# A hybrid decoder layer on one core: the merged blocks' sums change engine, low halves and transfers change place

## The chip, the cores and the metric

The kernel runs on one core of one Trainium2 chip. The metric is the device time of one execution in microseconds. Three timed runs of the kernel before stand beside one profiled execution, in which the hardware profiler recorded the instructions of every engine. The engines are TensorE (PE, with its weight loads PEld), VectorE (DVE), ScalarE (ACT), GpSimd (POOL) and SyncE (SP), whose queue starts nearly all DMAs here.

## The reference

One layer of a decoder with two token mixers side by side, 1024 tokens of width 1024, all in float32:

```python
h = rmsnorm(x, norm_g)
proj = h @ w_in                              # q, k, v, gates, decay code, merge logits
o_gla = gla_chunked(g_q, g_k, g_v, log_a)    # gated linear attention, 4 heads
o_gla = rmsnorm(o_gla, gla_norm_g) * silu(g_gate)
y_a = o_gla @ w_pa
o_sb = stick_breaking(s_q, s_k, s_v)         # 8 heads, strictly causal
o_sb = o_sb * silu(s_gate)
y_b = o_sb @ w_pb
gates = sigmoid(m_logits + b_gate)
merged = gates[0] * y_a + gates[1] * y_b
x = x + merged @ w_o
return rmsnorm(x, final_g)
```

The stick-breaking weight of key s for query t is beta[t, s] times the product of (1 - beta[t, j]) over s < j < t, with beta = sigmoid(q k / sqrt(d)).

## The kernel before, in words

**Numbers in two halves.** TensorE multiplies in a reduced form of float32. So every operand is split: ScalarE writes a high half (`activation(hi, src, Copy)`), VectorE subtracts it and writes a low half (`tensor_sub(lo, src, hi)`), and a product is three matmuls, high by high, high by low, low by high. The helper `split` (L164 to L166) does both; the last stage has its own, `o_hi` (L1188 on) and `o_lo` (L1192 on).

**Strassen blocks.** Large products are made from 2 x 2 blocks with seven products in place of eight, in Winograd's form: combinations S1 to S4 of one operand's blocks A11 to A22, combinations T1 to T4 of the other's blocks B11 to B22. A product of one unit is 12 matmuls of 128x512 (4 pieces of the contraction, three matmuls each).

**The stages, in order of time.**

1. The first rows of x are normalised (square on ScalarE, `norm_a`, with a first step of its reciprocal root on VectorE and the power on POOL; `norm_b` scales), transposed, split, and multiplied with the first value weights (L424 to L459). ScalarE and VectorE run in the order of the program here; the low halves of the first block are at L441, the low half of the first weights at L442.
2. Further values (L516 on), with the sums S1 to S4 of h.
3. "Pairs": 28 jobs of seven units (`Pairs.run`), each job a projection of 256 columns. While they run, other work is laid between the units: first the decay (22 slots), then the T sums of the two later weights w_pb and w_o (`tjobs`, L729 on: `t_load`, `t_sum`, `t_store`, one slot per unit), up to unit GLA_AT, then the GLA steps, four units to a step. TensorE's order is a scheduler's there; ScalarE's and VectorE's is the program's until the T sums end.
4. The stick-breaking heads (L1088 on), 8 heads of 8 steps. Step i of head h computes the scores of a later step, transposes the weights of block i (`turn`, tags tr and pp, high half ath or afh, low half atl or afl), and at two of the steps the values (`values`, bank av). Units of other projections are laid between by SB_PLAN. The order of all engines is a scheduler's.
5. The last stage (L1110 on), where ScalarE, VectorE and TensorE run in the order of the program: 28 items multiply the stick-breaking output by w_pb (`a_product`) and merge it with the other branch under the gates (`a_merge`), leaving merged blocks A11, A12, A21 and A22 in four quarters each; 28 further items multiply the merged blocks by w_o (`item`), add the residual (`add`), square for the norm (`square`), scale and store. An item is one product. I number them through, 0 to 55, so that 28 is the first of w_o.

**What sets the order in the last stage.** The table `parts` says at which item which operand is split, `loads` at which item which operand is loaded. In each item first the adds of finished products run (`evict_a`), then the low halves of this item (`los`), then the high halves of the next (`his`). Before the change, the merged sums S1, S3, S2 are made on POOL in the items 24 to 27 and S4 in 28 to 31 (`sums`, with `nc.gpsimd.tensor_tensor` in it, L1152); S4 and S3 go through DRAM (`d_s`) and come back by `o_load`. The low halves of A12 are made in the items 28 to 31, mixed with those of T2 and S2:

```python
28: [("T2", (0,)), ("A12", 0)], 29: [("T2", (1,)), ("A12", 1)], 30: [("S2", 0), ("S2", 1), ("A12", 2)],
31: [("A12", 3)], 33: [("S2", 2), ("S2", 3)], ...
```

The items 28 to 31 are A11 by B11, 32 to 35 A12 by B21, 36 to 39 S2 by T2, then S1 by T1 and S4 by B22 alternate (item 42 is the first of S4), 48 to 51 are S3 by T3 and 52 to 55 A22 by T4.

Of the kernel before, what the change touches and what calls it, by code (L numbers as in the profile page):

```python
# [15 lines left out]
P = 128  # L16
# [29 lines left out]
GLA_AT = 53  # L46
# [57 lines left out]
def hybrid_layer(ctx: ExitStack, tc: tile.TileContext, x, norm_g, w_in, w_up, b_dec,  # L104
# [35 lines left out]
    d_s = {nm: dram_set("s" + nm, 2, [P, 2, HALF]) for nm in ("S3", "S4", "A22")}  # L140
# [220 lines left out]
    with tc.tile_pool(name="p0", bufs=3, reuse_waits="tile") as p0:  # L361
# [62 lines left out]
        with tc.manual_schedule(engines={mybir.EngineType.Activation, mybir.EngineType.DVE}):  # L424
# [14 lines left out]
            norm_a(1)  # L439
            for g in range(2):  # L440
                nc.vector.tensor_sub(hq[0, g][1][:, :, 0:P], pts[g], hq[0, g][0][:, :, 0:P].bitcast(F32))  # L441
            nc.vector.tensor_sub(lo0, raw0, hi0.bitcast(F32))  # L442
# [268 lines left out]
    def t_load(k):  # L711
        wt[k] = tq.tile([P, 4, HALF], F32, tag="t", name="t")
        for two in range(2):
            rows = slice((2 * (k % 4) + two) * P, (2 * (k % 4) + two + 1) * P)
            if k < 4:
                for e in range(2):
                    nc.sync.dma_start(wt[k][:, 2 * two + e].rearrange("p (i c) -> p i c", c=P),
                                      w_pb[rows].rearrange("p (i e c) -> p e i c", e=2, c=P)[:, e])
            else:
                nc.sync.dma_start(wt[k][:, 2 * two:2 * two + 2], w_o[rows].rearrange("p (h c) -> p h c", h=2))  # L720
# [367 lines left out]
    for s, (h, i) in enumerate(steps):  # L1088
# [10 lines left out]
        if i == 0 and s:  # L1099
            values(h - 1, 1)  # L1100
        elif i == 5:
            values(h, 0)
# [41 lines left out]
    def sums(pre, js, nms):  # L1144

        for j in js:
            for nm in nms:
                x1, x2_, fn, where = {"S1": ("A21", "A22", ALU.add, None), "S3": ("A11", "A21", ALU.subtract, "A21"),
                                      "S2": ("S1", "A11", ALU.subtract, "A11"),
                                      "S4": ("A12", "S2", ALU.subtract, "A12")}[nm]  # L1150
                dst = oraw[pre + where, j] if where else mo_tile("A22" if pre == "" else "N", j)
                nc.gpsimd.tensor_tensor(dst, oraw[pre + x1, j], oraw[pre + x2_, j], op=fn)  # L1152
# [61 lines left out]
    sums("b", range(3), ("S1", "S3", "S2"))  # L1214
# [5 lines left out]
    sums("b", [3], ("S1", "S3", "S2"))  # L1220
# [3 lines left out]
    sums("b", ALL, ("S4",))  # L1224
# [68 lines left out]
    def y_load(n, t):  # L1293
        ys[n, t] = (sw.tile([P, D], F32, tag=("wh", "wl")[t % 2], name="y") if n == 0 else
                    py[0].tile([P, D], F32, tag="y", name="y"))
        r0 = n * HALF + t * P
        nc.sync.dma_start(ys[n, t], x2[r0:r0 + P, :])
# [14 lines left out]
    loads = {6: ("bB22", "tt"), 10: ("bT4",), 14: ("B11",), 16: ("B21", "tt"), 24: ("T2",), 26: ("T1",),  # L1312
             28: ("B22", "tt"), 34: ("S4",), 36: ("T3",), 39: ("S3", "tt"), 41: ("T4",), 43: ("A22",)}
# [16 lines left out]
    for k, it in enumerate(items):  # L1330
# [9 lines left out]
        if k >= 24:  # L1340
            y_load(0, k - 24)
            sums("", [k - 24], ("S1", "S3", "S2"))
# [15 lines left out]
    def add(n, t, J, bank):  # L1358
        nc.vector.tensor_add(ys[n, t][:, half(J)], bank, ys[n, t][:, half(J)])
# [115 lines left out]
```

## Time and profile before

| | us |
|---|---|
| three timed runs, median | 1220.27 |
| lowest and highest of them | 1218.0, 1220.41 |
| the profiled execution | 1220.52 |
| its span, from first to last instruction | 1218.8 |
| PE busy | 1190.8 |
| DVE busy | 849.3 |
| ACT busy | 556.1 |
| POOL busy | 343.0 |

Times inside the execution count from the start of its span. A row of the timeline has a start, a duration, an engine, a line of the code, the operation and what it writes and reads; in brackets stands how long the engine stood idle before it, and what ended that. Ends of matmuls are modelled: two that follow each other start 0.227 us apart, though each is shown as 0.39 long. A row of the waits has engine, line and what was waited for, then total us, times and the longest. A row of the groups has count, busy us and mean ns of one.

### The profile page before, as it was taken

Reading aid. Unit: us, or ns where it says so; the run is one execution under the profiler, and the core shown is the slowest. Engines: PE = TensorE matmul, PEld = TensorE weight load, DVE = VectorE, ACT = ScalarE, POOL = GpSimd, SP = SyncE. Lnnn points to the kernel's source line nnn. Section 1 sums busy time; section 2 is a strip of 40 time slices with the busy share of each in tenths; the row PEclk is TensorE's granted clock in tenths of the full one; section 3 lists DMA queues with packets and bytes.
Section 4 is the critical chain, followed back from the end, with each engine's and each line's share of the span. In section 5 each row is a group of like instructions: output and inputs, shape, how many; then the busy total and the mean of one; then the engine's idle time right before and its main releaser. Section 6 shows DMA issues by size and latency. Waiting matters only on the chain.

```text
span 1218.8 us, 17307 instructions
## 1 busy us (share of the span) xinstructions
PE 1190.8 (98%) x6087; PEld 1000.3 (82%) x6087; DVE 849.3 (70%) x1323; ACT 556.1 (46%) x1079; POOL 343.0 (28%) x319
## 2 busy tenths in 40 slices
PE   8999999999999999999999999999999999999797
PEld 8999878877888888888888887888887888788586
DVE  5575876786757667867666528777677874579876
ACT  5344663234335445444444325554456553374243
POOL 1495523142422322422423202111121111602601
PEclk9999999999999999999999999999999999999899
DMA  7544349976656646656655187545877547649562
GB/s 278 186 142 141 147 168 343 373 276 199 198 156 195 190 146 208 212 189 218 209 165 170 65 276 241 179 161 180 286 265 245 179 141 276 212 160 301 172 240 105
DMA packets 205652, 249.77 MB, mean 205 GB/s; under 512 B 12503, under 2 KB 141549, under 8 KB 203005
## 3 DMA queue, kind: packets, MB, share of 16 engines
q1 hardware_dynamic: 204988, 247.62, 61.7%
q8 instruction: 48, 0.79, 0.3%
q10 hardware_dynamic: 576, 1.05, 0.2%
q14 instruction: 40, 0.32, 0.1%
HBM read 155.30 MB, written 93.32 MB: 204 GB/s over the span
## 4 chain that ended last, share of the span: by engine, by line
PE 79%; DVE 9%; DMA 6%; ACT 3%; issue 2%; SPq 1%; POOL 0%; ACTq 0%; DVEq 0%; POOLq 0%
PE pp L270 12%; PE pp L272 12%; PE pp L271 12%; PE pp L223 8%; PE pp L204 4%; PE pp L205 4%; PE pp L206 4%; DMA f<-d_e 2%; PE av L1002 1%; PE z L955 1%; PE av L1001 1%; PE av L1000 1%; PE tr L979 1%; DMA raw<-in_w_in_dram 1%; PE z L957 1%
## 5 line engine op out<-in xcount | busy, mean ns | idle before, releaser
L964 POOL TENSOR_SCALAR_AFFINE_SELECT be<-be 128x128 f32<-128x128 f32 x64 | 40.4, 633 | 232.3 <-ACT be L960 221.1
L166 DVE TENSOR_TENSOR wl<-tt,wh 128x1024 fp32r<-128x1024 f32 x56 | 70.2, 1253 | 50.4 <-ACT wh L165 50.0
L244 POOL TENSOR_TENSOR tt<-raw 128x512 f32<-128x512 f32 x28 | 39.2, 1400 | 212.9 <-DVE wl L166 208.6
L309 DVE TENSOR_TENSOR f<-pp,f 128x512 f32<-128x512 f32 x84 | 57.7, 688 | 58.8 <-PE pp L272 58.1
L963 DVE TENSOR_TENSOR_SCAN eb<-eb,m 128x128 f32<-128x128 f32 (+3 forms) x64 | 86.5, 1353 | 9.5 <-ACT eb L959 9.5
L165 ACT ACTIVATE wh<-tt 128x1024 fp32r<-128x1024 f32 x56 | 59.3, 1059 | 68.8 <-PE pp L271 68.2
L165 ACT ACTIVATE wh<-raw 128x1024 fp32r<-128x1024 f32 x47 | 49.7, 1060 | 80.7 <-PE pp L271 39.5
L166 DVE TENSOR_TENSOR wl<-raw,wh 128x1024 fp32r<-128x1024 f32 x47 | 67.9, 1445 | 25.0 <-ACT wh L165 20.1
L276 ACT ACTIVATE f<-pp 128x512 f32<-128x512 f32 x84 | 49.6, 591 | 71.9 <-PE pp L272 70.5
L231 POOL TENSOR_TENSOR r<-r,nhalf 128x1 f32<-128x1 f32 x40 | 24.3, 607 | 188.5 <-DVE r L230 178.3
L959 ACT ACTIVATE eb<-z 128x384 f32<-128x384 f32 (+4 forms) x96 | 49.0, 511 | 36.7 <-issue 23.9
L967 DVE TENSOR_TENSOR be<-be,eb 128x128 f32<-128x128 f32 (+3 forms) x64 | 48.8, 763 | 3.2
L960 ACT ACTIVATE be<-z 128x384 f32<-128x384 f32 (+4 forms) x96 | 49.4, 515 | 0.0
L270 PE MATMUL pp<-ha11h,wh 128*128 128x512 f32 x112 | 44.8, 400 | 2.6 <-ACT wh L165 2.6
L270 PE MATMUL pp<-S3h,wh 128*128 128x512 f32 x112 | 45.0, 401 | 0.0
L270 PE MATMUL pp<-ha22h,wh 128*128 128x512 f32 x112 | 44.5, 397 | 0.2 <-DVE f L309 0.2
L270 PE MATMUL pp<-ha12h,wh 128*128 128x512 f32 x112 | 44.5, 397 | 0.0
L270 PE MATMUL pp<-S1h,wh 128*128 128x512 f32 x112 | 44.5, 397 | 0.0
L271 PE MATMUL pp<-S3l,wh 128*128 128x512 f32 x112 | 44.1, 394 | 0.0
L272 PE MATMUL pp<-S3h,wl 128*128 128x512 f32 x112 | 44.1, 394 | 0.0
L270 PE MATMUL pp<-S4h,dh 128*128 128x512 f32 x112 | 44.0, 392 | 0.0
L270 PE MATMUL pp<-S2h,wh 128*128 128x512 f32 x112 | 43.9, 392 | 0.0
(510 smaller groups left out, 4007.9 us busy)
## 6 DMA issues: line engine op xcount, KB each, us to landing
raw<-in_w_in_dram SPq DMA_DIRECT2D x31, 1024.0 KB, 6.4
d_v<-o SPq DMA_DIRECT2D x32, 256.0 KB, 3.0
d_gv<-o SPq DMA_DIRECT2D x32, 256.0 KB, 4.0
d_t<-t SPq DMA_DIRECT2D x8, 1024.0 KB, 5.5
v<-d_gv SPq DMA_DIRECT2D x32, 256.0 KB, 3.3
d_ogl<-o SPq DMA_DIRECT2D x64, 128.0 KB, 2.5
d_q<-o SPq DMA_DIRECT2D x16, 512.0 KB, 3.9
d_k<-o SPq DMA_DIRECT2D x16, 512.0 KB, 4.1
```

The costliest lines, as they stand in the source:

```text
L165: nc.scalar.activation(hi, src, AF.Copy)
L166: eng.tensor_sub(lo, src, hi.bitcast(F32))
L223: nc.tensor.matmul(pt[:, 0:n], *ops[kb][i], start=k == 0, stop=k == 3 * KB - 1)
L270: nc.tensor.matmul(pt, bh[:, j], ah[:, j], start=first and j == 0, stop=False, skip_group_check=True)
L271: nc.tensor.matmul(pt, bh[:, j], al[:, j], start=False, stop=False, skip_group_check=True)
L272: nc.tensor.matmul(pt, bl[:, j], ah[:, j], start=False, stop=j == 3, skip_group_check=True)
L276: nc.scalar.activation(t[nm], t[bank], AF.Copy)
L309: nc.vector.tensor_add(add, bank, add)
L959: nc.scalar.activation(om[:, osl], zt[:, 0:w], AF.Sigmoid, scale=-inv_sqrt)
L960: nc.scalar.activation(be[:, osl], zt[:, 0:w], AF.Sigmoid, scale=inv_sqrt)
L963: nc.vector.tensor_tensor_scan(rest, rest, m1[:, off:T][:, ::-1], 1.0, op0=ALU.mult, op1=ALU.max)
L967: nc.vector.tensor_mul(be[:, off:T], be[:, off:T], om[:, off + 1:T + 1])
```

## The change

Six things are edited.

- The merged sums run on VectorE (`sums` gets the engine as an argument), placed by a new table `merged`: S1 and S2 of quarter j behind the low halves of item 28 + j, S4 in the items 33 to 36, S3 in 37 to 40. S2 is written in the place of A22 instead of A11. S4 is split straight from where it stands; only S3 still goes through DRAM.
- The low halves of A12 come first, two quarters in item 28 and two in 29; T2 moves to 30 and 31, S2 to 32 and 33. `loads` follows.
- The x rows of the second half are loaded by halves in item 30 (three of four) and 41, in other tiles, in place of item 37.
- The T sums' transfers go by halves: each block is loaded in two slots and stored in two, and blocks start 3 slots apart instead of 2.7. GLA_AT goes from 53 to 56, so that three more units stand before the GLA steps and three fewer behind them.
- In the first stage the low halves of the first block move ahead of `norm_a(1)`, whose square runs on ScalarE.
- `values(h, 0)` moves from step 5 of a head to step 4.

```diff
-GLA_AT = 53
+GLA_AT = 56
...
             keep_warm(WARM[1])
-            norm_a(1)
             for g in range(2):
                 nc.vector.tensor_sub(hq[0, g][1][:, :, 0:P], pts[g], hq[0, g][0][:, :, 0:P].bitcast(F32))
+            norm_a(1)
...
-    def t_store(k):
-        nc.sync.dma_start(d_t[k][:], wt[k])
+    def t_store(k, i):
+        nc.sync.dma_start(d_t[k][:, 2 * i:2 * i + 2], wt[k][:, 2 * i:2 * i + 2])
...
-        at = 27 * k // 10
-        tjobs[at].append((t_load, (k,)))
+        at = 3 * k
+        for i in range(2):
+            tjobs[at + i].append((t_load, (k, i)))
+            tjobs[at + 9 + i].append((t_store, (k, i)))
         for i in range(4):
             tjobs[at + 6 + i // 2].append((t_sum, (k, i)))
-        tjobs[at + 9].append((t_store, (k,)))
...
-        if i == 0 and s:
-            values(h - 1, 1)
-        elif i == 5:
-            values(h, 0)
+        if i % 4 == 0 and s:
+            values(*((h, 0) if i else (h - 1, 1)))
...
-                                      "S2": ("S1", "A11", ALU.subtract, "A11"),
+                                      "S2": ("S1", "A11", ALU.subtract, "A11" if pre else "A22"),
...
-                nc.gpsimd.tensor_tensor(dst, oraw[pre + x1, j], oraw[pre + x2_, j], op=fn)
+                eng.tensor_tensor(dst, oraw[pre + x1, j], oraw[pre + x2_, j], op=fn)
...
+             28: [("A12", 0), ("A12", 1)], 29: [("A12", 2), ("A12", 3)], 30: [("T2", (0,))], 31: [("T2", (1,))],
...
+    merged = {**{28 + j: (j, ("S1", "S2")) for j in range(4)}, **{33 + j: (j, ("S4",)) for j in range(4)},
+              **{37 + j: (j, ("S3",)) for j in range(4)}}
...
+        if k in merged:
+            j, nms = merged[k]
+            sums("", [j], nms, nc.vector)
+            if nms == ("S3",):
+                nc.sync.dma_start(d_s["S3"][j // 2][:, j % 2], oraw.pop(("S3", j)))
...
-            sums("", [k - 24], ("S1", "S3", "S2"))
...
-        if 3 <= k < 7:
-            for nm in ("S4", "S3"):
-                nc.sync.dma_start(d_s[nm][(k - 3) // 2][:, (k - 3) % 2], oraw[nm, k - 3])
...
-        if k < 4:
-            sums("", [k], ("S4",))
...
-        if k == 9:
+        if k == 2:
+            for t in range(3):
+                y_load(1, t)
+        if k == 13:
             mo_ctx.close()
...
-            for t in range(4):
-                y_load(1, t)
+            y_load(1, 3)
```

More of the change, by code (lines that the diff above doesn't have):

```diff
@@ L139, in hybrid_layer @@
     d_t = dram_set("t", 8, [P, 4, HALF])
-    d_s = {nm: dram_set("s" + nm, 2, [P, 2, HALF]) for nm in ("S3", "S4", "A22")}
+    d_s = {nm: dram_set("s" + nm, 2, [P, 2, HALF]) for nm in ("S3", "A22")}
     ident = const.tile([P, P], F32, tag="ident", name="ident")
@@ L709, in hybrid_layer, with t_load @@
     tq = tq_ctx.enter_context(tc.tile_pool(name="tq", bufs=4, reuse_waits="tile"))
[L711 to L714, printed above, removed]
-            if k < 4:
[L716 to L720, printed above, removed]
+    def t_load(k, two):
+        if two == 0:
+            wt[k] = tq.tile([P, 4, HALF], F32, tag="t", name="t")
+        rows = slice((2 * (k % 4) + two) * P, (2 * (k % 4) + two + 1) * P)
+        if k < 4:
+            for e in range(2):
+                nc.sync.dma_start(wt[k][:, 2 * two + e].rearrange("p (i c) -> p i c", c=P),
+                                  w_pb[rows].rearrange("p (i e c) -> p e i c", e=2, c=P)[:, e])
+        else:
+            nc.sync.dma_start(wt[k][:, 2 * two:2 * two + 2], w_o[rows].rearrange("p (h c) -> p h c", h=2))
     def t_sum(k, i):
@@ L1223, in hybrid_layer @@
     o_split("bB21", AB)
-    sums("b", ALL, ("S4",))
+    sums("b", ALL, ("S4",), nc.gpsimd)
     o_load("bT3")
@@ L1293, in y_load @@
     def y_load(n, t):
[L1294 to L1295 removed]
+        if n == 0 or t < 2:
+            y = sw.tile([P, D], F32, tag=("wh", "wl")[t % 2], name="y")
+            ys[n, t] = [y[:, half(J)] for J in range(2)]
+        elif t == 2:
+            ys[n, t] = [sw.tile([P, 4, P], F32, tag="d" + e, name="yd", bufs=1).rearrange("p a c -> p (a c)")
+                        for e in "hl"]
+        else:
+            y = py[0].tile([P, D], F32, tag="y", name="y")
+            ys[n, t] = [y[:, half(J)] for J in range(2)]
         r0 = n * HALF + t * P
[L1297 removed]
+        for J in range(2):
+            nc.sync.dma_start(ys[n, t][J], x2[r0:r0 + P, half(J)])
     parts = {0: [("bS2", 0), ("bS2", 1)], 1: [("bS2", 2), ("bS2", 3)], 2: [("bT2", (0,))], 3: [("bT2", (1,))],
@@ L1364, in square @@
         junk = ps.tile([P, HALF], F32, tag="av", name="junk", bufs=1)
-        nc.scalar.activation(junk, ys[n, t][:, half(J)], AF.Square, accum_out=ssq[:, i, J:J + 1])
+        nc.scalar.activation(junk, ys[n, t][J], AF.Square, accum_out=ssq[:, i, J:J + 1])
     def factor(n, t, J):
```

24 lines of the change are left out of this document (10 added, 14 removed), and 10 rows, old and new, of the table parts.

## The prediction

> **What bounds the kernel now.** I read the page first, then TensorE's waits, then the windows and the timeline around each wait.
>
> ```profile
> PE 1190.8 (98%) x6087; PEld 1000.3 (82%) x6087; DVE 849.3 (70%) x1323; ACT 556.1 (46%) x1079; POOL 343.0 (28%) x319
> ```
>
> TensorE (PE) is busy for 98% of the span, so a change can win only what PE loses: waits, and matmuls that run at a lower clock. TensorE's waits name the losses (total us, times, longest):
>
> ```profile
> PE pp L1353 <- DVE A12l L1194: 7.5, 3, 4.0
> PE pp L270 <- ACT wh L165: 2.6, 1, 2.6
> PE tr L979 <- DVE atl L166: 2.1, 2, 1.5
> PE pp L223 <- DVE ha11l L441: 1.4, 1, 1.4
> PE pp L223 <- DVE vw L442: 0.7, 1, 0.7
> PE pp L979 <- DVE be L967: 0.7, 1, 0.7
> ```
>
> Each has its own place. In the windows (length, busy PE, PEld, DVE, ACT, POOL, then the granted clock, DMA share, GB/s) the first row holds the four products of A12 and B21 in the last stage, the second the 20 products after them:
>
> ```profile
> 1135.96:1157.46 21.50, 14.03 (x50) 10.32 (x49) 17.13 (x19) 5.11 (x10) 11.91 (x8) 0.76 0.39 139
> 1157.46:1212.00 54.54, 54.54 (x241) 44.86 (x239) 41.35 (x63) 23.51 (x42) 3.85 (x7) 1.00 0.47 167
> ```
>
> The 20 take 54.54 / 20 = 2.727 us each, without a gap. The four should take 10.91 and took 21.50: 10.59 us lost, 7.5 of it waits and the other 3.1 the lower clock (0.76) behind them. This is the largest loss, and VectorE (DVE) causes it. Groups there (count | busy us, mean ns), the first two and the POOL row from 1118 to 1150, the fourth from after 1150:
>
> ```profile
> L1194 DVE TENSOR_TENSOR A12l<-A,A12h 128x512 fp32r<-128x512 f32 x4 | 7.0, 1762 | 0.0
> L1359 DVE TENSOR_TENSOR y<-xb,y 128x512 f32<-128x512 f32 x4 | 2.6, 676 | 0.0
> L1152 POOL TENSOR_TENSOR A<-A,A 128x512 f32<-128x512 f32 x12 | 20.4, 1710 | 1.3 <-DVE A12l L1194 0.7
> ...
> L1194 DVE TENSOR_TENSOR S1l<-A,S1h 128x512 fp32r<-128x512 f32 x4 | 2.6, 685 | 0.0
> ```
>
> While POOL makes the 16 merged sums, a low half on DVE with two SBUF operands takes 1.76 us; after them an equal one takes 0.685. An add that reads PSUM keeps its 0.68 throughout. So POOL and DVE hinder each other over SBUF, DVE falls behind, and the low halves of A12 come late:
>
> ```profile
> 1121.34 2.31 DVE L1194 TENSOR_TENSOR B11l<-raw,B11h 128x1024 fp32r<-128x1024 f32 x1
> ...
> 1131.45 2.31 DVE L1194 TENSOR_TENSOR T2l<-raw,T2h 128x1024 fp32r<-128x1024 f32 x1
> 1133.68 1.77 DVE L1194 TENSOR_TENSOR A12l<-A,A12h 128x512 fp32r<-128x512 f32 x1
> ...
> 1144.43 0.80 PE L1353 MATMUL pp<-B21h,A12l 128*128 128x512 f32 x1 [4.05 <-DVE A12l L1194]
> ```
>
> **The change part by part.**
>
> **Merged sums and A12.** VectorE's order at this place, from the second half of B21, before and then changed (A with a number is a merged quarter, N the merged A22):
>
> ```order
> L1194 TENSOR_TENSOR B21l<-tt,B21h 128x1024
> L1194 TENSOR_TENSOR T2l<-raw,T2h 128x1024
> L1194 TENSOR_TENSOR A12l<-A_10895,A12h 128x512
> L1194 TENSOR_TENSOR T2l<-raw,T2h 128x1024
> L1194 TENSOR_TENSOR A12l<-A_10917,A12h 128x512
> L1194 TENSOR_TENSOR S2l<-A_10523,S2h 128x512
> L1194 TENSOR_TENSOR S2l<-A_10541,S2h 128x512
> L1194 TENSOR_TENSOR A12l<-A_10939,A12h 128x512
> ```
>
> ```order
> L1193 TENSOR_TENSOR B21l<-tt,B21h 128x1024
> L1193 TENSOR_TENSOR A12l<-A_10901,A12h 128x512
> L1193 TENSOR_TENSOR A12l<-A_10923,A12h 128x512
> L1151 TENSOR_TENSOR A_11093<-A_10990,N 128x512
> L1151 TENSOR_TENSOR N<-A_11093,A_10529 128x512
> L1193 TENSOR_TENSOR A12l<-A_10945,A12h 128x512
> L1193 TENSOR_TENSOR A12l<-A_10967,A12h 128x512
> L1151 TENSOR_TENSOR A_11117<-A_11016,N 128x512
> ```
>
> The four A12l move ahead of T2 and S2, and the sums (L1151) stand between them. Is DVE still in time with 16 more instructions? What a DVE instruction costs in a row of them is the distance between starts:
>
> ```profile
> 1163.70 1.28 DVE L1194 TENSOR_TENSOR S1l<-A,S1h 128x512 fp32r<-128x512 f32 x2
> 1164.91 1.22 DVE L1194 TENSOR_TENSOR B22l<-tt,B22h 128x1024 fp32r<-128x1024 f32 x1
> 1166.04 0.69 DVE L1359 TENSOR_TENSOR y<-xb,y 128x512 f32<-128x512 f32 x1
> ```
>
> Two of 512 take 1.21 (0.605 each), one of 1024 takes 1.13. Before, DVE reached T2l at 1131.45. Three of the 1024-wide ahead of it (one B11l, two B21l) took about 2.31 where 1.22 would do; without POOL it gets there 3.3 us earlier, about 1128.2. Two A12l, two sums, two A12l: six times 0.605, done at 1131.8. PE opens its first product with A12 at 1135.96, so some 4 us are to spare and the wait goes whole. What is late next? From the first A12l to the S3 sum of item 40, DVE has 43 instructions of 512 (8 A12l and S2l, 4 S1l, 2 S4l, 16 sums, 13 adds), 6 of 1024 (T2, T1, B22) and a few tiny ones: 26.0 + 6.8 + 0.8 = 33.6, so it is through at 1161.8, where PE ends item 41 (28 + 13) at 1125.05 + 14 x 2.727 = 1163.2. DVE then adds that product and makes the last two S4l in 1.8 us; PE wants the first of these 8 matmuls (1.8 us) into item 42. It just fits. A further lag costs PE its own length there; I count nothing. S4 loses its way through DRAM (4 stores and 2 loads on SP's queue); S3 still goes that way, and its load is wanted at item 48, 19 us later. New waits: ScalarE's high halves of S2 and S4 wait for DVE's sums, made an item or more ahead, with squares and high halves of later items queued behind; SP's S3 stores wait for DVE as well, and behind them stand the loads of S3 and A22. The x loads move from item 37 to item 30: 6 issues, behind which SP has only loads that are wanted 4 and more items on. Gain: **10.6 us**.
>
> **The odd matmul at 249 us.** TensorE's order among the paired projections, before and then changed (S1, S3 and ha11 are the combinations of h that a product reads):
>
> ```order
> L271 MATMUL pp<-S1l,wh 128x512
> L272 MATMUL pp<-S1h,wl 128x512
> L270 MATMUL pp<-ha11h,wh 128x512
> L270 MATMUL pp<-S3h,wh 128x512
> L271 MATMUL pp<-S3l,wh 128x512
> ```
>
> ```order
> L270 MATMUL pp<-S1h,wh 128x512
> L271 MATMUL pp<-S1l,wh 128x512
> L272 MATMUL pp<-S1h,wl 128x512
> L270 MATMUL pp<-S3h,wh 128x512
> L271 MATMUL pp<-S3l,wh 128x512
> ```
>
> Before, the scheduler put one matmul of the next job ahead of S3; after, that job begins behind the 36 matmuls of S3, S4 and ha22. Nothing in the diff names this: the shifted weight sums and GLA_AT let the scheduler decide otherwise. What the odd one cost:
>
> ```profile
> 246.41 0.39 PE L272 MATMUL pp<-S1h,wl 128*128 128x512 f32 x1
> 248.28 1.04 ACT L165 ACTIVATE wh<-raw 128x1024 fp32r<-128x1024 f32 x1
> 249.37 0.58 PE L270 MATMUL pp<-ha11h,wh 128*128 128x512 f32 x1 [2.57 <-ACT wh L165]
> 249.85 0.79 PE L270 MATMUL pp<-S3h,wh 128*128 128x512 f32 x1
> 253.00 0.43 PE L271 MATMUL pp<-S3l,wh 128*128 128x512 f32 x1
> ```
>
> PE stood 2.57 us for a high half that ScalarE had at 249.3. Then seven steps took 253.00 - 249.85 = 3.15 where 7 x 0.227 = 1.59 is usual: 1.56 more. In the new order S3 goes on at 246.8 and the high half is wanted 36 x 0.227 = 8.2 us later, at 255, with 5.7 to spare. If the half came that late too, the wait would be back. Gain: **4.1 us**. The halved transfers themselves change no wait of PE; eight more stores on SP lie under PE's work.
>
> **Low halves ahead of the square.**
>
> ```profile
> 8.20 0.73 DVE L437 CAST vw<-raw 128x1088 fp32r<-128x1088 f32 x1 [0.30 <-DMA raw<-in_w_in_dram]
> 10.56 0.15 DVE L230 TENSOR_SCALAR r<-ssq 128x1 f32<-128x1 f32 x1 [1.64 <-ACT xs L389]
> 11.83 1.28 DVE L442 TENSOR_TENSOR vw<-raw,vw 128x1088 fp32r<-128x1088 f32 x1
> ```
>
> DVE idled 1.64 us for the square, then made two low halves, then L442. Now the two fill 8.9 to 10.2, r still comes at 10.56, and L442 starts at 10.63: 1.2 earlier. PE stands at L442's result. Gain: **1.2 us**. Behind it:
>
> ```profile
> 7.30:10.60 3.30, 2.67 (x21) 2.25 (x20) 1.36 (x3) 2.35 (x4) 0.00 (x0) 1.00 1.10 372
> 10.60:14.00 3.40, 1.87 (x10) 1.43 (x11) 3.40 (x6) 2.26 (x3) 0.55 (x1) 1.00 1.03 422
> 14.00:17.40 3.40, 3.40 (x18) 3.40 (x17) 2.31 (x4) 0.60 (x1) 0.55 (x1) 0.52 1.02 417
> ```
>
> A window with 1.87 us of PE work in 3.40 is followed by one at clock 0.52, one with 2.67 in 3.30 is not. The change lifts the 1.87 to about 2.4, between the two: 0 or 1.7 us more; I take 0.
>
> **Values one step earlier.** The diff also moves values(h, 0) from step 5 to step 4 of each head. TensorE's order in the third head, before and changed (tr and pp are transposes of a block of be, av the values):
>
> ```order
> L979 MATMUL tr<-ident,be 128x128
> L979 MATMUL pp<-ident,be 128x128 x4
> L955 MATMUL z<-k,q 128x512
> L956 MATMUL z<-k,q 128x512
> L957 MATMUL z<-k,q 128x512
> L979 MATMUL tr<-ident,be 128x128
> L955 MATMUL z<-k,q 128x512
> L956 MATMUL z<-k,q 128x512
> L957 MATMUL z<-k,q 128x512
> L979 MATMUL tr<-ident,be 128x128
> L979 MATMUL pp<-ident,be 128x128 x4
> L1000 MATMUL av<-ath,v 128x512
> ```
>
> ```order
> L980 MATMUL tr<-ident,be 128x128 x4
> L956 MATMUL z<-k,q 128x448
> L957 MATMUL z<-k,q 128x448
> L958 MATMUL z<-k,q 128x448
> L956 MATMUL z<-k,q 128x448
> L957 MATMUL z<-k,q 128x448
> L958 MATMUL z<-k,q 128x448
> L980 MATMUL tr<-ident,be 128x128
> L980 MATMUL pp<-ident,be 128x128 x4
> L1001 MATMUL av<-ath,v 128x512
> L1002 MATMUL av<-atl,v 128x512
> ```
>
> The scores and transposes of the next block no longer stand between step 4's transposes and av, and av's second matmul reads the low half (atl) of block 3. The transposes of step 4, and when DVE began that low half, in the first, fifth and last head of the eight:
>
> ```profile
> 749.02 0.60 PE L979 MATMUL pp<-ident,be 128*128 128x128 f32 x4
> 750.36 0.68 DVE L166 TENSOR_TENSOR atl<-tr,ath 128x512 fp32r<-128x512 f32 x1
> ...
> 887.28 0.60 PE L979 MATMUL pp<-ident,be 128*128 128x128 f32 x4
> 890.16 0.68 DVE L166 TENSOR_TENSOR atl<-tr,ath 128x512 fp32r<-128x512 f32 x1
> ...
> 992.44 0.60 PE L979 MATMUL pp<-ident,be 128*128 128x128 f32 x4
> 992.93 0.68 DVE L166 TENSOR_TENSOR atl<-tr,ath 128x512 fp32r<-128x512 f32 x1
> ```
>
> PE would want the half 0.6 after the first time and have it 0.68 after the second: waits of 1.4, 3.0 and 0.6 us, over the eight pairs 7.9. Against it stand the 2.1 + 0.7 = 2.8 us that PE already waits for atl and be here and that would fall into the same pause. So +5.1 at most, -2.8 at best. I take the middle, **+1.2**: a PE that has waited once in a head is late against DVE for the rest of it.
>
> A rule speaks to these waits. The Trainium skill, "TensorE: Matmul & The Clock Gate", Part 1, lets the clock fall to half after one idle window of about 3.4 us; by it a wait of 3.0 us would cost only itself. The rows above disagree: 2.57 us idle were enough at 249 us, and 1.5 us in a window of 3.4. So the longest of these waits may bring 1.6 more, which I keep for the upper end. By the skill's rule rival 2 below would be 1209.4 instead of 1211.
>
> **GLA_AT and the rest.** Three paired units move from behind the GLA steps to before them, so the reload of h's fourth quarter has less cover:
>
> ```profile
> ha21h<-d_a SPq DMA_DIRECT2D x1, 1024.0 KB, 6.5
> ```
>
> It may go when S2's last product is read; until its use stand S1, three units (8.2 us) and the first gate product (24 matmuls, 5.4), 16 us against 6.5 for landing. Nothing; were the cover gone, PE would wait at the second gate product for what is missing.
>
> Sum: 10.6 + 4.1 + 1.2 - 1.2 = 14.7. The profiled execution took 1220.52 (span 1218.8, 1.7 around it), so 1205.8; the runs' median lies 0.25 lower: **1205.5 us**.
>
> **The rivals.**
> 1. *The wait at 249 us comes back elsewhere*, since the late DVE that caused it is still late. For it: PE's order is one of many. Against: 5.7 us to spare. 1205.5 + 4.1 = 1209.6.
> 2. *The values wait in full*: +5.1 instead of +1.2, and the lower clock once: 1205.5 + 3.9 + 1.6 = 1211.
> 3. *Slower: DVE, not POOL, is the trouble.* If the 1.76 us came from where the blocks lie in SBUF, the 16 sums would pay it too, and DVE would bound items 28 to 41. It decides there: DVE's 33.6 us may grow by 1.9 (to the 35.5 that PE needs for 13 items) + 4.2 (the lead before A12) + 14.7 (all gains) = 21 before the kernel loses; with 30 such instructions and six double ones, 42 in all, that is 0.5 us each, from 1.1 us per sum. At 1.76 they take 42 x 1.155 = 48 more: 1220.3 + 48 - 21 = about 1247. Against it: the adds from PSUM stayed at 0.68 and the low halves fell to 0.685 when POOL ended.
>
> **How the numbers follow.** The forecast has 0.62, rival 1 0.14, rival 2 0.2, rival 3 0.03, no change 0.01. Below the forecast lie the values at -2.8 and the window at full clock, 1199.8 together and 1201.5 for one of them; above it rival 2. Range 1201.5 to 1211. A measurement of this kernel tells 0.2%, 2.4 us, from no change; all but rival 3 gain far more: faster 0.96, same 0.01, slower 0.03.
>
> **What would show it.** Right: no wait of L1353's successor for A12l, all products of the last stage 2.727 us apart at clock 1.00, low halves at 0.69 throughout; no slow window near 250; L442 at about 10.6. Wrong: waits at av for atl of over 5 us in total, S4's product waiting for its low half, merged sums on DVE at over 1 us each.

## The result, and the profile after

| | before | after |
|---|---|---|
| median of the timed runs, us | 1220.16 (4 runs) | 1203.74 (4 runs) |
| lowest and highest | 1218.0, 1220.41 | 1202.95, 1205.73 |
| the profiled execution | 1220.52 | 1205.73 |
| its span | 1218.8 | 1204.0 |

The ratio after to before is 0.9872, with a 95% interval of 0.9855 to 0.9889: 16.4 us by the medians, 14.8 us between the two profiled executions. After's profiled execution is the slowest of its four runs. The forecast was 1205.5 for the median and 1205.8 for the profile.

Where the 14.8 us came from can be read from the starts of a few matmuls of TensorE (PE) in the timelines. The lead is before minus after, the gain what a stage adds to it:

| PE starts with | before | after | lead | gain of the stage ahead |
|---|---|---|---|---|
| the paired projections | 115.78 | 115.62 | 0.16 | first stage and values: 0.16 |
| the first projection laid into the heads (L204) | 725.08 | 719.74 | 5.34 | paired stage: 5.18 |
| the first merged product (xa) | 1048.16 | 1043.65 | 4.51 | heads: -0.83 |
| item 28 | 1125.08 | 1120.56 | 4.52 | 28 items of w_pb: 0.01 |
| its last matmul | 1211.63 | 1196.50 | 15.13 | 28 items of w_o: 10.61 |
| (end of the span) | 1218.8 | 1204.0 | 14.8 | behind PE: -0.33 |

The page of after, then PE's waits (engine, line, what was waited for: total us, times, longest):

```profile
PE 1185.2 (98%) x6087; PEld 997.8 (83%) x6087; DVE 855.4 (71%) x1341; ACT 555.8 (46%) x1081; POOL 316.7 (26%) x303
```

```profile
PE av L1002 <- DVE atl L166: 3.1, 3, 1.5
PE z L956 <- ACT be L961: 1.6, 4, 0.7
PE warm L149 <- POOL ident masks.py:199: 1.4, 1, 1.4
PE pp L223 <- DVE vw L442: 1.3, 1, 1.3
```

The first two lines of before, 7.5 us for A12l and 2.6 for the weights' high half wh, are gone. The largest new line, 3.1 us of av for atl, stands where the values were moved; none of its three waits is longer than 1.5 us. The windows of after, items 32 to 39 and then 40 to the end (length, busy PE, PEld, DVE, ACT, POOL, clock, DMA share, GB/s):

```profile
1131.40:1153.20 21.80, 21.80 (x97) 18.03 (x97) 20.97 (x35) 11.91 (x22) 0.00 (x0) 1.00 0.33 109
1153.20:1196.90 43.70, 43.69 (x193) 35.85 (x191) 35.18 (x56) 16.91 (x32) 3.84 (x7) 1.00 0.40 143
```

Eight products in 21.80 are 2.725 us each, at full clock. VectorE (DVE) in front of them:

```profile
1123.31 1.28 DVE L1193 TENSOR_TENSOR A12l<-A,A12h 128x512 fp32r<-128x512 f32 x2
1124.51 0.68 DVE L1151 TENSOR_TENSOR A<-A,N 128x512 f32<-128x512 f32 x1
1125.22 0.69 DVE L1151 TENSOR_TENSOR N<-A,A 128x512 f32<-128x512 f32 x1
1125.83 1.29 DVE L1193 TENSOR_TENSOR A12l<-A,A12h 128x512 fp32r<-128x512 f32 x2
```

A merged sum takes 0.69, the four A12l are done at 1127.1, and PE wants the first at 1131.4: 4.3 us to spare, forecast 4.2. The paired stage no longer has the odd matmul; PE goes from S1 to S3 without a gap:

```profile
246.19 0.39 PE L272 MATMUL pp<-S1h,wl 128*128 128x512 f32 x1
246.42 0.39 PE L270 MATMUL pp<-S3h,wh 128*128 128x512 f32 x1
```

In the first stage L442 came 1.05 us earlier for PE (13.16 before), but the next transposes then waited for xs:

```profile
12.11 0.52 PE L223 MATMUL pp<-vw,ha11h 128*128 128x272 f32 x2 [1.27 <-DVE vw L442]
...
13.40 1.08 PE L419 MATMUL tr<-ident,xs 128*128 128x128 f32 x4 [0.27 <-DVE xs L399]
```

So far the sum agrees with the forecast's, though the paired stage gained more than the 4.1 us that were forecast and the first stage less than the 1.2. The experiments ask whether the reasons hold.

### The profile page after: what moved, and what is told of

It reads as the page before. It is cut to its first block, busy times and chain, and to the rows that moved or that the text cites. A ratio compares the mean times of both kernels' runs of the same rounds, so it can differ in the third digit from the quotient of the medians.

```text
span 1204.0 us, 17310 instructions
## 1 busy us (share of the span) xinstructions
PE 1185.2 (98%) x6087; PEld 997.8 (83%) x6087; DVE 855.4 (71%) x1341; ACT 555.8 (46%) x1081; POOL 316.7 (26%) x303
## 3 DMA queue, kind: packets, MB, share of 16 engines
q10 hardware_dynamic: 576, 1.05, 0.2%
## 4 chain that ended last, share of the span: by engine, by line
PE 83%; DVE 7%; DMA 3%; ACT 3%; issue 3%; SPq 1%; POOL 0%; DVEq 0%; ACTq 0%
PE pp L270 12%; PE pp L272 12%; PE pp L271 12%; PE pp L223 8%; PE pp L204 4%; PE pp L206 4%; PE pp L205 4%; PE av L1002 2%; PE av L1003 1%; PE z L956 1%; PE av L1001 1%; PE tr L980 1%; PE xb L1368 1%; PE xb L1367 1%; PE z L957 1%
## 5 line engine op out<-in xcount | busy, mean ns | idle before, releaser
L309 DVE TENSOR_TENSOR f<-pp,f 128x512 f32<-128x512 f32 x84 | 57.8, 688 | 59.1 <-PE pp L272 55.7
L166 DVE TENSOR_TENSOR wl<-raw,wh 128x1024 fp32r<-128x1024 f32 x47 | 70.5, 1501 | 22.4 <-ACT wh L165 21.6
L271 PE MATMUL pp<-ha22l,wh 128*128 128x512 f32 x112 | 43.7, 390 | 0.0
L272 PE MATMUL pp<-ha22h,wl 128*128 128x512 f32 x112 | 43.7, 390 | 0.0
```

What stands on the lines that cost most here:

```text
L166: eng.tensor_sub(lo, src, hi.bitcast(F32))
L271: nc.tensor.matmul(pt, bh[:, j], al[:, j], start=False, stop=False, skip_group_check=True)
L272: nc.tensor.matmul(pt, bl[:, j], ah[:, j], start=False, stop=j == 3, skip_group_check=True)
L309: nc.vector.tensor_add(add, bank, add)
```

## The experiments

Twelve kernels ran, each an edit of before or of after. The paired stage, the heads and w_o are the stretches between the starts in the table above, each in the kernel's own profile, which is one execution; the ratio is to the kernel before, timed beside it, whose medians there were 1220.15 to 1220.96. Code that is the same in a stage gives an idea of the spread of these stretches: the paired stage takes 603.90 to 604.71 in the six kernels that have after's code there and 608.06 to 609.30 in the three that have before's, and w_o takes 86.55 to 87.72 in before, b_ldq and b_nosum.

| kernel | median us | ratio, 95% interval | paired | heads | w_o |
|---|---|---|---|---|---|
| before | 1220.16 | | 609.30 | 323.08 | 86.55 |
| after | 1203.74 | 0.9872 (0.9855 to 0.9889) | 604.12 | 323.91 | 75.94 |
| a_pool: after, sums on POOL | 1204.02 | 0.9868 (0.9855 to 0.9882) | 603.90 | 323.17 | 76.71 |
| b_dve: before, sums on DVE | 1218.32 | 0.9985 (0.9975 to 0.9994) | 608.94 | 322.96 | 84.87 |
| b_order: before, A12 first | 1210.26 | 0.9911 (0.9893 to 0.9929) | 608.06 | 322.59 | 77.91 |
| a_whole: after, T in whole blocks | 1206.30 | 0.9892 (0.9876 to 0.9907) | 606.18 | 324.11 | 75.94 |
| a_whole53: that, old slots, GLA_AT 53 | 1208.84 | 0.9902 (0.9883 to 0.9921) | 608.58 | 321.74 | 75.93 |
| a_g53: after, old slots, GLA_AT 53 | 1209.71 | 0.9909 (0.9891 to 0.9927) | 610.78 | 323.33 | 75.93 |
| b_ldq: before, decay loads from POOL | 1217.21 | 0.9971 (0.9958 to 0.9984) | 604.61 | 322.12 | 87.22 |
| b_nosum: before without T sums | 1213.79 | 0.9943 (0.9929 to 0.9958) | 603.51 | 322.70 | 87.72 |
| a_val5: after, values at step 5 | 1204.23 | 0.9870 (0.9857 to 0.9883) | 604.71 | 323.27 | 75.93 |
| a_sq: after, square first | 1204.45 | 0.9864 (0.9839 to 0.9888) | 603.99 | 323.86 | 75.94 |
| a_warm: after, filled pause | 1204.96 | 0.9865 (0.9848 to 0.9883) | 604.00 | 324.95 | 75.93 |
| b_min: before, two edits | 1206.18 | 0.9875 (0.9859 to 0.9892) | 603.96 | 324.53 | 76.75 |

### The last stage: which half of the edit pays

**Sums back on POOL (a_pool).**

```diff
-            sums("", [j], nms, nc.vector)
+            sums("", [j], nms, nc.gpsimd)
```

> The changed kernel with its merged sums back on POOL, at the same places in the program and with the same tiles. Theory (POOL and VectorE hinder each other over SBUF, and A12's low halves only had to come first): VectorE's low halves that run beside the sums (second pair of A12, T2, S2, S4) take about 1.7 us again and a sum on POOL 1.7, but A12 is through before 1131.4 all the same (two at 0.69 by 1124.5, two at 1.76 by about 1129.5), so TensorE does not wait for it; the eight sums S1 and S2 take 13.7 us from about 1124 and are done at 1138, ahead of the first S2 product at 1142.3. Time 1204 to 1208, at most 4 us above the changed kernel. Rival 3 of the prediction (the place of the blocks makes 1.76 us): low halves stay at 0.69 here too, since every tile lies as in the changed kernel. Rival 'the engine is what counted': the wait for A12 is back with its slow window and the time is about 1214.

Time and ratio are those of after. DVE's row of the four A12l, then PE's one wait in the stage:

```profile
1124.46 6.87 DVE L1193 TENSOR_TENSOR A12l<-A,A12h 128x512 fp32r<-128x512 f32 x4
```

```profile
1137.74 0.50 PE L1366 MATMUL pp<-B21h,A12h 128*128 128x512 f32 x1 [0.41 <-DVE y L1374]
```

All four A12l took 6.87 / 4 = 1.72 us, not only two: POOL isn't held to the program's order here and began its sums at 1111.72, 12.7 us ahead of them. They were done at 1131.33. Item 32 starts at 1118.08 + 4 x 2.725 = 1128.98 and reads the fourth low half as its last matmul, 2.5 us later, at 1131.5. So the slow instructions just fit, and PE lost 0.41 us for a bank. That refutes rival 3 (every tile lies as in after, and 0.64 becomes 1.72 per instruction by the engine alone) and it refutes something of the forecast too: the wait for A12l is gone without the sums leaving POOL.

**The engine alone (b_dve).**

```diff
-    def sums(pre, js, nms):
+    def sums(pre, js, nms, eng=nc.gpsimd):
...
-                nc.gpsimd.tensor_tensor(dst, oraw[pre + x1, j], oraw[pre + x2_, j], op=fn)
+                eng.tensor_tensor(dst, oraw[pre + x1, j], oraw[pre + x2_, j], op=fn)
...
-            sums("", [k - 24], ("S1", "S3", "S2"))
+            sums("", [k - 24], ("S1", "S3", "S2"), nc.vector)
...
-            sums("", [k], ("S4",))
+            sums("", [k], ("S4",), nc.vector)
```

> The kernel before with its merged sums on VectorE, in the same places of the program (items 24 to 31), and nothing else changed. Theory (engine and order are needed together): low halves at 0.69 throughout, but 12 sums of 0.605 (7.3 us) now stand in front of T2l and save only 3 x 1.1 there, so T2l starts 4 us later than 1131.45; the A12 halves, mixed with T2, S2, S4 sums and adds, are done at about 1143 to 1144, TensorE waits 5 to 7 us for them in place of 7.5, and the slow window stays: 1217 to 1220, at most 3 us below before. Rival 'the engine alone does it': no wait for A12, 1209.6.

The time is as expected. DVE's group of A12l, then PE's rows with a wait in the A12 products:

```profile
L1194 DVE TENSOR_TENSOR A12l<-A,A12h 128x512 fp32r<-128x512 f32 x4 | 2.7, 685 | 0.0
```

```profile
1136.63 0.50 PE L1353 MATMUL pp<-B21h,A12l 128*128 128x512 f32 x1 [0.53 <-DVE A12l L1194]
1139.10 0.50 PE L1353 MATMUL pp<-B21h,A12l 128*128 128x512 f32 x1 [1.49 <-DVE A12l L1194]
1141.63 0.79 PE L1353 MATMUL pp<-B21h,A12l 128*128 128x512 f32 x1 [1.30 <-DVE A12l L1194]
1144.16 0.80 PE L1353 MATMUL pp<-B21h,A12l 128*128 128x512 f32 x1 [0.88 <-DVE A12l L1194]
```

The low half is at 0.685 and still late: the last A12l is made at 1143.42, behind T2, S4 sums and adds. PE waits 4.2 us, and the clock halves behind waits of which none is longer than 1.5. The engine alone is worth 1.7 us of w_o's 10.6 in this profile, with low halves as fast as after's.

**The order alone (b_order).**

```diff
-             28: [("T2", (0,)), ("A12", 0)], 29: [("T2", (1,)), ("A12", 1)], 30: [("S2", 0), ("S2", 1), ("A12", 2)],
-             31: [("A12", 3)], 33: [("S2", 2), ("S2", 3)], 34: ...
+             28: [("A12", 0), ("A12", 1)], 29: [("A12", 2), ("A12", 3)], 30: [("T2", (0,))], 31: [("T2", (1,))],
+             32: [("S2", 0), ("S2", 1)], 33: [("S2", 2), ("S2", 3)], 34: ...
```

> The kernel before with the low and high halves of A12 first (items 28, 29), T2 in 30 and 31, S2 in 32 and 33; the merged sums stay on POOL in the items 24 to 31. Theory (the order alone moves the wait on): VectorE reaches the first A12l at 1131.45 and makes four at 1.72 (POOL still sums), done at 1138.3, just when the first A12 product reads the fourth (1138.5), so that wait goes; two T2l at 2.31, adds and four S2l at 1.72 follow and are done at 1149.5 (two) and about 1153 (all), where the first S2 product wants them at 1147 to 1149: TensorE waits 3 to 5 us there, with a slow window behind it or not: 1212 to 1217. Rival (the order alone is the gain): no wait, 1209.6. Rival (contention alone is the cause): wait for A12l as before, 1219 to 1220.

```profile
1129.86 6.88 DVE L1194 TENSOR_TENSOR A12l<-A,A12h 128x512 fp32r<-128x512 f32 x4
...
1147.65 1.28 DVE L1194 TENSOR_TENSOR S2l<-A,S2h 128x512 fp32r<-128x512 f32 x2
```

```profile
1144.30 0.50 PE L1351 MATMUL pp<-B21h,A12h 128*128 128x512 f32 x1 [1.56 <-DVE y L1359]
```

My theory fell here: the wait did not move on to S2. POOL was through at 1146.5, the last two S2l ran at 0.64 and were done at 1148.9, in time. Swapping table entries gives 86.55 - 77.91 = 8.64 of the 10.61 us in this profile. In b_min (below), whose last stage is the same code, it gives 86.55 - 76.75 = 9.80: the wait for an add, 1.56 us here, is 0.4 there. So the order is worth 8.6 to 9.8, and the sums' new engine and places 0.8 to 2.0. In a_pool, with the sums at their new places but on POOL, 9.84 of the 10.61 are there.

### The paired stage: what made the wait at 249 us

**Whole transfers (a_whole).** Slots and GLA_AT are those of after.

```diff
-    def t_store(k, i):
-        nc.sync.dma_start(d_t[k][:, 2 * i:2 * i + 2], wt[k][:, 2 * i:2 * i + 2])
+    def t_store(k):
+        nc.sync.dma_start(d_t[k][:], wt[k])
...
-            tjobs[at + i].append((t_load, (k, i)))
-            tjobs[at + 9 + i].append((t_store, (k, i)))
+            tjobs[at].append((t_load, (k, i)))
...
+        tjobs[at + 9].append((t_store, (k,)))
```

> The changed kernel with the transfers of the T sums whole again (a load in one slot, a store in one), GLA_AT and the slots as in the changed kernel. The scheduler then puts two matmuls of the next job ahead of S3 near 249 us again, where before it put one. Theory (the order of TensorE there is what cost 4.1 us): TensorE stands about 2.6 us for the high half of the weights near 249 and runs a window at half clock behind it: 1207.8. Rival (the high half itself came late because of the transfers or of VectorE's sums, and order is nothing): no wait, 1203.7.

```profile
244.93 0.39 PE L270 MATMUL pp<-ha11h,wh 128*128 128x512 f32 x1
245.16 0.39 PE L271 MATMUL pp<-ha11l,wh 128*128 128x512 f32 x1
245.38 0.39 PE L270 MATMUL pp<-S3h,wh 128*128 128x512 f32 x1
...
252.66 0.50 PE L270 MATMUL pp<-ha22h,wh 128*128 128x512 f32 x1 [1.68 <-DVE f L309]
```

The odd matmul is back, as two, and costs nothing: ScalarE had the high half at 244.1. A wait stands at another product instead (1.68 us, for a bank that DVE drains at L309) and one at a transpose (0.55 at 263.9). The median, 1206.30, lies between what the theory and the rival gave. The order on PE decides where a late DVE shows, not whether. The forecast's reason for its 4.1 us, the order, fails here.

**The whole edit of T undone (a_whole53), and only slots and GLA_AT undone (a_g53).**

```diff
-GLA_AT = 56
+GLA_AT = 53
...
-        at = 3 * k
+        at = 27 * k // 10
```

a_whole53 has this on top of a_whole's edit, a_g53 has it alone.

> The changed kernel with the whole edit of the T sums undone: whole transfers, blocks 2.7 slots apart, GLA_AT 53. Theory (what cost 2.6 + 1.5 us near 249 was VectorE waiting for the loads of the decay, which stand on SP's queue behind whole blocks of T; the place of the odd matmul only decides which product shows it): VectorE waits about 6 us in sum for those loads, TensorE stands 2 to 2.6 us for the weights' high half near 248, and the paired stage takes 608 to 609.3 us in place of 604: 1207.5 to 1209. Rival (the lead of the first stage removed it): no wait there, 1204 to 1206.5.

> The changed kernel with halved transfers, but blocks 2.7 slots apart and GLA_AT 53 as before. Two matmuls of the next job stand ahead of S3 again. Theory (halves let the loads of the decay through sooner): VectorE waits 3 to 4.5 us in sum for them, TensorE has no wait of 2 us for the weights near 249: 1203.5 to 1206. Rival (the wider slots did it): the wait is back, 1207.5 to 1209.

PE's waits near 249 in a_whole53, then in a_g53:

```profile
246.97 0.51 PE L270 MATMUL pp<-ha11h,wh 128*128 128x512 f32 x1 [1.40 <-ACT wh L165]
254.44 0.50 PE L270 MATMUL pp<-ha22h,wh 128*128 128x512 f32 x1 [1.25 <-DVE f L309]
```

```profile
250.28 0.80 PE L270 MATMUL pp<-ha11h,wh 128*128 128x512 f32 x1 [3.92 <-ACT wh L165]
```

The first is as expected in the median (1208.84) and in the stage (608.58, in the fastest of its five executions), with 1.40 + 1.25 us there and 0.88 at 274.9. The second is the slowest of all in the stage, against my expectation. By these profiles the wider slots gain 608.58 - 606.18 = 2.4 us with whole blocks; halves gain 606.18 - 604.12 = 2.1 with the wider slots, and cost 610.78 - 608.58 = 2.2 with the old ones. The medians agree with the two gains (2.5 and 2.6 us) but show only 0.9 of the cost, with intervals that overlap nearly whole. So halves pay with the wider slots, in the profile clearly and in the timed runs with intervals that overlap in part; that they do harm with the old ones is not shown.

Two waits go with the arrangement, both from 180 to 262 us: DVE's for the decay's loads (f from d_e, L562), and SP's, ahead of a load of T (L720), for an earlier block to be stored (d_t). The rows of before, then of a_g53, and all five in a table:

```profile
DVE f L562 <- DMA f<-d_e: 5.9, 3, 3.5
SPq L720 <- DMA d_t<-t: 2.9, 1, 2.9
```

```profile
DVE f L562 <- DMA f<-d_e: 10.0, 3, 4.1
SPq L720 <- DMA d_t<-t: 8.8, 4, 4.8
```

| us | DVE waits for the decay's loads | SP waits for a store of T | paired stage |
|---|---|---|---|
| after | 2.7 | none | 604.12 |
| a_whole53 | 4.2 | 2.1 | 608.58 |
| before | 5.9 | 2.9 | 609.30 |
| a_whole | 7.2 | 3.1 | 606.18 |
| a_g53 | 10.0 | 8.8 | 610.78 |

The two waits rank alike: while SP's queue stands for a tile of T to become free, the decay's loads behind it are not issued. There are four tiles, so block k + 4 takes the tile of block k, 10 or 11 slots later in the old arrangement and 12 in the new; the second half of a halved store is issued in slot 10, which with the old slots leaves one slot or none. That fits the 8.8 of a_g53, but not the 3.1 of a_whole, where three slots are left. No run with more tiles tests it. Nor do the waits rank the stage alone: a_whole waits longer for loads than a_whole53 and loses less.

**The decay's loads from POOL's queue (b_ldq), and no T sums (b_nosum).** In before DVE waits 3.5 us for such a load, until 241.65, and then has two T sums, a low half and two T sums beside POOL (5 us) ahead of L309. ScalarE's o (L569) waits for what L309 writes, and the weights' high half, for which PE stands at 249, follows o on ScalarE. DVE's rows of before, then ScalarE's:

```profile
241.65 0.69 DVE L562 SCALAR_TENSOR_TENSOR f<-pp,f 128x512 f32<-128x512 f32 x1 [3.52 <-DMA f<-d_e]
242.26 1.41 DVE L724 TENSOR_TENSOR t<-t 128x512 f32<-128x512 f32 x2
243.59 1.22 DVE L166 TENSOR_TENSOR wl<-tt,wh 128x1024 fp32r<-128x1024 f32 x1
244.72 2.38 DVE L724 TENSOR_TENSOR t<-t 128x512 f32<-128x512 f32 x2
247.03 0.68 DVE L309 TENSOR_TENSOR f<-pp,f 128x512 f32<-128x512 f32 x1
...
247.74 0.63 ACT L569 ACTIVATE o<-f 128x512 f32<-128x512 f32 x1 [6.39 <-DVE f L309]
```

The two edits, b_ldq's first:

```diff
-                nc.sync.dma_start(es[J, n], d_e[2 * i + J][:, half(n)])
+                nc.gpsimd.dma_start(es[J, n], d_e[2 * i + J][:, half(n)])
```

```diff
-        for i in range(4):
-            tjobs[at + 6 + i // 2].append((t_sum, (k, i)))
```

> The kernel before, with the loads of the decay (f from d_e) started by POOL in place of SP, so that they no longer stand behind the blocks of T; nothing else changed. Theory (series: VectorE is late at 247 because the load landed 3.5 us late and two T sums, a low half and two slow T sums, 5 us, follow it; taking away either is enough for the 2.57 us): VectorE's wait for these loads falls from 5.9 to under 3 us, the wait near 249 and most of that near 277 go, the paired stage takes 604 to 606 us in place of 609.3: 1215 to 1217. Rival (the loads don't matter, VectorE's own work sets the pace): 608 to 609.5 us, 1219 to 1220.

> The kernel before without the 32 T sums on VectorE (they are left out of the computation; blocks are loaded and stored unchanged). Theory (series): the loads of the decay come as late as before (VectorE waits 5 us or more for them), but the bank is drained 3.8 us earlier, so the waits near 249 and 277 go: paired stage 604 to 605.5 us, 1215 to 1216. Rival (the late loads alone make the wait): wait near 249 as before, 1218.5 to 1220.

In b_ldq DVE has no wait at L562 for a DMA, and the longest wait of PE behind 200 us in the stage is this:

```profile
271.49 0.66 PE L605 MATMUL tr<-ident,f 128*128 128x128 f32 x4 [0.45 <-DVE f L309]
```

In b_nosum DVE waits for the loads as long as before, and PE has neither the wait near 249 nor the one near 277, though two matmuls of the next job stand ahead of S3 (at 247.88) as in a_whole:

```profile
DVE f L562 <- DMA f<-d_e: 6.3, 4, 2.8
```

Both paired stages fall to what after has (604.61 and 603.51). So it was a series: a late load and DVE's own sums behind it, and taking away either is enough. In b_ldq PE's order had changed as well (no odd matmul), but a_whole and b_nosum show that the odd one alone costs nothing. The medians miss what was expected, b_ldq's by 0.2 us above its range and b_nosum's by 1.2 below.

### The heads and the first stage

**Values at step 5 (a_val5).**

```diff
-        if i % 4 == 0 and s:
-            values(*((h, 0) if i else (h - 1, 1)))
+        if i == 0 and s:
+            values(h - 1, 1)
+        elif i == 5:
+            values(h, 0)
```

> The changed kernel with the first values of a head back at step 5. Theory (the earlier step costs what the lead lost between 725 and 1048 us, 5.4 to 4.5): TensorE's waits in the heads fall from 5.4 to about 4.2 us and the time by 0.9 us, to about 1202.9; the wait of av for the low half of block 3 (3.1) is gone and one of the transposes for it is back. Rival (the lead was lost to something else there): the same waits in sum, or more, and the time within 0.5 us of the changed kernel or above it.

PE's waits from 717 to 1045 us, a_val5 and then a_pool, which has after's code in the heads:

```profile
PE tr L980 <- DVE atl L166: 2.4, 2, 1.5
PE z L956 <- ACT be L961: 1.8, 4, 0.9
PE pp L980 <- DVE be L968: 0.7, 1, 0.7
PE tr L980 <- DVE be L968: 0.3, 1, 0.3
```

```profile
PE av L1002 <- DVE atl L166: 3.1, 3, 1.5
PE z L956 <- ACT be L961: 1.8, 4, 0.9
PE pp L980 <- DVE be L968: 0.5, 1, 0.5
PE tr L980 <- DVE be L968: 0.3, 1, 0.3
```

The sums are 5.2 and 5.7: the waits change names, and half a microsecond separates them. The heads take 323.27 and 323.17, and other kernels with one step or the other lie between 321.74 and 324.95. Nothing can be told from this move, neither the 1.2 that I counted nor the 0.9 I then expected.

**Square first (a_sq), and the pause filled (a_warm).**

```diff
             keep_warm(WARM[1])
+            norm_a(1)
             for g in range(2):
                 nc.vector.tensor_sub(hq[0, g][1][:, :, 0:P], pts[g], hq[0, g][0][:, :, 0:P].bitcast(F32))
-            norm_a(1)
```

```diff
+            for _ in range(8):
+                nc.tensor.matmul(warm[:, 0:P], hq[0, 1][1][:, 3, 0:P], hq[0, 1][0][:, 3, 0:P], start=True, stop=True)
             norm_a(1)
```

> The changed kernel with norm_a(1) ahead of the first low halves again. Theory (this edit, by filling TensorE's pause, is what keeps the clock up in the first stage in three of four profiles): the waits of 1.4 and 0.7 us and the window at half clock near 14 us are back, the paired stage starts at 115.7 in place of 114.1: about 1205.3. Rival (the window comes and goes by itself): start of the pairs between 114 and 115.8 in either kernel, time within 0.5 us of the changed kernel.

> The changed kernel with eight small matmuls (128x128, the result isn't used) laid into TensorE's pause of 1.27 us ahead of L442 in the first stage. Theory (the window at half clock there follows a window that TensorE does not fill): the window is gone in every run, pairs start at 114.1 or up to 0.3 earlier; median 0 to 0.7 below the changed kernel, 1203.0 to 1203.7. Rival (the window does not depend on the fill): still there in the profile or in a quarter of the runs, and the eight matmuls cost up to 0.5: 1203.7 to 1204.5.

The ratios of both are after's; a_sq's median, 1204.45, lies between its two expectations, and a_warm's, 1204.96, above both of its ranges. The pairs begin at 115.66 in each, with the window at half clock. In after, a_pool, a_val5, a_whole, a_whole53 and a_g53, whose first stage is the same code, they begin at 115.62 in after (with the window) and at 113.9 to 114.1 in the five others (without). a_warm moved its wait to the next operand:

```profile
12.11 0.39 PE L223 MATMUL pp<-vw,ha11h 128*128 128x272 f32 x1 [0.40 <-DVE vw L444]
13.40 0.77 PE L419 MATMUL tr<-ident,xs 128*128 128x128 f32 x4 [0.90 <-DVE xs L399]
```

So the window, some 1.5 us, comes and goes with one and the same code. With the low halves first it is in 2 of 7 profiles (after and a_warm), with the square first in 6 of 7 (all but b_ldq). That the edit makes it rarer is likely but not shown; the medians of a_sq and after don't differ measurably.

### Two edits alone (b_min)

The table entries of b_order and after's transfers, slots and GLA_AT, on the kernel before.

> The kernel before with two edits alone: A12 first (as in the run with the order alone) and the transfers and slots of the T sums with GLA_AT 56. Merged sums on POOL in the items 24 to 31, square first, values at step 5, x rows at item 37 as before. Theory (these two carry nearly all): 1210.3 - 5.0 = 1205.3, between 1204.5 and 1206. Rival (the edits need each other or the rest): 1207 to 1210.

1206.18, just above the expected range, beside runs of before that were 0.8 us longer in that job; as a ratio 0.9875 against 0.9872 for the whole change. These two edits carry all that can be measured. The sums' engine, S4 without DRAM, the x rows, the square and the values together lie within the intervals. The traces tell one thing more finely: with the sums on POOL, w_o takes 76.71 (a_pool) and 76.75 (b_min), 0.8 us more than after's 75.94. No kernel here is measurably faster than after.

## Why the prediction was right, and where its reasons were not

- **Merged sums and A12, 10.6 us.** Measured 10.61 in the items of w_o, with 4.3 us to spare and sums at 0.69, as worked out. That POOL and DVE hinder each other holds (0.64 against 1.72 per low half on the same tiles). But the forecast priced two edits as one, and made the slow instructions the cause. b_order, b_min and a_pool show that the order pays 8.6 to 9.8 of it with the slow instructions still there, and b_dve that fast ones in the old order pay 1.7. The Trainium skill, "SBUF — State Buffer", section "SBUF: two separate sides", lets one of the two engines block the other for a whole instruction when VectorE's has two SBUF inputs and GpSimd's reads SBUF. The 1.72 of a_pool agrees in kind, and says nothing about whether the time is on PE's path.
- **The odd matmul at 249 us, 4.1 us.** The wait is gone, the paired stage gained 5.2. The step "Nothing in the diff names this: the shifted weight sums and GLA_AT let the scheduler decide otherwise" took the order for the cause, and "The halved transfers themselves change no wait of PE" priced the cause at nothing. a_whole and b_nosum have the odd matmul and no wait there. DVE was late, from a load of the decay on SP's queue and T sums behind it (b_ldq, b_nosum), and transfers and slots together relieve it: undoing the halves alone brings 2.1 us of the stage back (a_whole). The wait of 0.9 at L605 near 277, which stands in before's list of waits and which the forecast neither showed nor counted, goes with the same two edits (b_ldq leaves 0.45 of it, b_nosum none), which makes most of the difference between 4.1 and 5.2. Rival 1 had the right thought (the late DVE is the cause), but that lateness was what the change removed. That the wait went at all was luck, by the forecast's own reason for it.
- **Low halves ahead of the square, 1.2 us.** PE had L442 1.05 us earlier, and 0.16 was left at 115.6. The scaling of the next rows (xs) had not come earlier by as much, so PE waited 0.27 for it and stood 0.61 ahead at 13.4; a further 0.5 went by 28.6, where the second weights' high half had moved behind a square on ScalarE. The step that counted the 1.2 as the stage's gain stopped at the first wait. The window, taken at 0 of "0 or 1.7", stayed in after's profile, and is missing in most profiles of the same code. That is likely why the median lies 2.0 under the profile; after's other runs have no trace to show it.
- **Values one step earlier, +1.2 us.** In after's profile the heads are 0.83 longer, near the value taken, but a_pool and a_val5 show it to be spread; that agreement is luck. Neither end of the range (+5.1, -2.8) came; rival 2 is out.
- **The rest, 0.** b_min confirms it for the sums' transfers, the x rows and S4. The end behind PE is 0.33 longer in the profile; the last transfer is issued 3.65 after PE's last matmul in both.

The total was right because the sum was made from measured losses, which the change did remove, and because the windfalls and shortfalls nearly cancelled: +1.1 in the paired stage, -1.0 in the first, +0.4 in the heads, -0.3 at the end. That they cancel to 0.1 us in the profile is luck; the median came 1.8 us lower than forecast.

## What to carry to other kernels

Before crediting a faster engine, ask whether the late operand was merely late in the queue: here swapping table entries gave 8.6 to 9.8 of 10.6 us with every slow instruction in place. Where a scheduler's odd order meets a wait, follow the releaser back through its own queue to a transfer; the order tells where lateness shows, the queue why. An edit that spreads transfers has to be weighed with their spacing: halves gained 2.1 us of the stage at the wider one, and at the other nothing that the timed runs could tell (a loss of 2.2 in the one profile).

## What the runs showed of the hardware that I had not expected

- POOL's sums slow DVE in the paired stage too: a T sum (0.69 by itself) beside POOL's four weight sums takes 1.74, two of them 3.48, in after as in a_whole.

```profile
243.27 3.48 DVE L724 TENSOR_TENSOR t<-t 128x512 f32<-128x512 f32 x2
```

- Two short waits close together halved the clock: in b_dve the waits of 0.53 and 1.49 us, which ended at 1136.63 and 1139.10 with three matmuls between them, were followed by 0.50 from 1139.65 on, before the third wait began at 1140.3, and for 10.2 us. A single wait of 1.56 us in b_order and one of 1.68 in a_whole left the clock at 1.00.

```profile
1139.65:1149.85 10.20, 8.02 (x18) 5.30 (x17) 7.06 (x13) 1.76 (x4) 0.00 (x0) 0.50 0.50 170
```

- One code, two clocks: the first stage of after and of a_pool, from 13.0 us on, at 0.55 and at 1.00.

```profile
13.00:16.50 3.50, 3.23 (x15) 3.13 (x15) 2.84 (x5) 1.17 (x3) 0.55 (x1) 0.55 1.03 420
```

```profile
13.00:16.40 3.40, 2.87 (x22) 2.58 (x21) 2.69 (x5) 1.66 (x5) 0.55 (x1) 1.00 1.03 420
```

The Trainium skill, "TensorE: Matmul & The Clock Gate", Part 1, says that the window in which the gate measures is free-running and does not begin with the kernel. That could give these two; no run here shows where the window's edges lay.
